# A hybrid recurrent layer with sixteen experts: the second expert's token gather placed ahead of the overflow branch

## The chip, the cores and the metric

The kernel runs on one core of a Trainium2 chip. The metric is the device time of one execution, in microseconds. Engines are named as in the profile: PE (TensorE, its weight loads PEld apart), DVE (VectorE), ACT (ScalarE), POOL (GpSimd) and SP (SyncE, which here issues most DMAs).

## The reference

One layer over 512 latent tokens of 1024 channels (and 256 context tokens that only feed the recurrences): a modulated norm, an input projection, two groups of four recurrent heads, an output projection with a gated residual, and then a mixture of sixteen experts, of which each token takes the two best of its best group of four. A final norm follows. The part around the change is this:

```python
xs = xs + g1x * (ox @ w_out[l])
xs = xs + g2x * hierarchical_moe(modulate(rms_norm(xs, norm2_w[l]), sh2x, sc2x), *moe_args)
...
g_idx = jnp.argmax(g_logits, axis=-1)
top_v, top_i = lax.top_k(e_in_group, TOP_K_IN_GROUP)
expert_id = g_idx[:, None] * EXPERTS_PER_GROUP + top_i
...
for e in range(N_EXPERTS):
    a = jax.nn.silu(t @ w_gate[e]) * (t @ w_up[e])
    y = y + gates[:, e:e + 1] * (a @ w_down[e])
...
return rms_norm(xs, final_norm_w)
```

Everything is float32. The expert weights are 16 x 3 matrices of 2 MB.

## The kernel before

**Stages.** Up to about 545 us the kernel makes the modulation, the input projection and the two recurrences. The output projection runs in two halves of 512 channels: the first (L1278) for all four token tiles of 128, the second (L1336) tile by tile. Behind each tile of the second half DVE adds the residual (`residual`, L1219 to L1236; the add is L1224), PE turns the tile channel-major and makes the 20 router logits (L1250), and DVE adds and scales them (L1254, L1255). `Routing.route` (L99) picks the two experts of each token and their positions in the experts' lists, for tiles 0 and 1 first and then for tiles 2 and 3.

**Token rows.** `token_rows(t)` (L1260 to L1269) makes the normed and modulated rows of tile t in two DVE instructions (a multiply L1266 by the broadcast `a2`, a multiply-add L1267 with `sh2`) and writes them to `t_d`, a buffer in device memory, in one DMA of 512 KB (L1268). Tiles 0 and 1 are made during the output projection and written from SP's queue; tiles 2 and 3 are made later and written from POOL's queue (`t >= RA`, RA is 2).

**Slot tables.** `Routing.finish` (L198) builds the table that says which token sits in which of 128 slots of each expert: eight one-hot tiles on DVE (`collect`, L176), eight small matmuls into `s0ps` (L177), and five short DVE instructions (`table`, L182 to L186) that end in the row numbers.

**Expert 0** takes its tokens by matmuls with one-hots (L1290, L1296), then gets its scale and shift in `x0` (L1408 on DVE, L1410 on ACT), and runs the gate and up products in float32 (L1424). All other experts take their tokens by an indirect DMA (`gather`, L1370 to L1373) from `t_d`: it needs all four tiles of rows and the table. The gather of expert 1 is L1371 on POOL.

**The overflow branch.** The largest count of tokens of an expert is loaded into a register (L1431), and `tc.If(over > P)` (L1432) branches over a loop for experts with more than 128 tokens. Every engine takes part in the branch, and where it is skipped each engine's queue still raises the semaphores that the skipped code would have raised. `branch` (L1477) is the branch's place in the program; weight loads written after it are held behind it.

**Experts 1 to 15.** `up(e)` transposes the gathered rows on PE (L1501), splits them into a high and a low part (`xh` on ACT, `xl` on DVE), and makes gate (`pg`) and up (`pu`) products of 24 reduced-precision matmuls each (L1513). `down(e)` does the same for the down projection (`at` L1531, `ah` on ACT L1535, `al` on DVE L1536, `py` L1544). The weights are split the same way, high on ACT (L1393) and low on DVE (L1398), into four buffers each. `gated` (L1524) is the activation between them; the first one after the branch needs a table load on ACT. `down` of expert e-1 stands between the two products of expert e.

**Weight loads.** `load_weights` (L1198 to L1207) issues 96 loads of 1 MB from SP's queue in the order of a list, `(expert, piece)` with pieces 0 and 1 gate, 2 and 3 up, 4 and 5 down. The raw tiles rotate through 12 buffers of three pools (a string, `turns`, says which). Ten loads are issued ahead of the branch, five in the output projection and five after the mixer's buffers are free; three more stand right behind the branch in the program, and the rest as buffers come free.

**What sets the order.** A scheduler places instructions on the engines by priority and dependencies. `tc.issue_after(i)` and `tc.add_manual_dep(..., behind, ...)` keep an instruction behind another in the order, and `hi(1000)` raises priority. The two late broadcast loads, `g2b` (the gate of the second residual, L1488) and `fw` (the final norm's weight, L1490), 512 KB each, reuse the buffers of `a2` and `sh2`, and so wait until the last token rows are made.

## Time and profile before

| | |
|---|---|
| median of 3 runs | 979.87 us (977.32 to 984.05) |
| the profiled execution | 978.06 us |
| its span, first to last instruction | 976.3 us |
| mean granted TensorE clock | 0.958 of full speed |
| PE busy | 875.8 us (90%) |
| PEld busy | 717.4 us (73%) |
| DVE busy | 732.7 us (75%) |
| ACT busy | 499.6 us (51%) |
| POOL busy | 216.4 us (22%) |
| DMA moved | 180.03 MB, mean 184 GB/s |

Times in the trace are counted from the start of the span. The profiled execution is 1.8 us longer than its span, and 1.8 us below the median. In rows of the timeline a bracket gives the idle time of the engine in front of the instruction and what ended it; in rows of windows the numbers are the window, its length, the busy time and instruction count of PE, PEld, DVE, ACT and POOL, the granted clock, the busy share of the DMA engines and GB/s. A clock of 1.00 is 2.4 GHz, 0.50 is 1.2 GHz.

### The profile page before, as it was taken

The page shows a single profiled execution, that of the slowest core. Times are in us where ns is not written, and L with a number is a line of the kernel's source. Part 1 is how long each engine was busy: PE and PEld are TensorE (multiplying, and loading weights), DVE is VectorE, ACT ScalarE, POOL GpSimd, SP SyncE. Part 2 cuts the span into 40 slices and gives each one's busy share as a digit, 9 for nine tenths or more (in the row PEclk, how much of TensorE's full clock was granted, in tenths as well). Part 3 has the DMA queues.
Part 4 walks back from the last instruction along what each step waited for, and adds up shares of the span by engine and source line. Part 5 has one row for each costly group of instructions (what it writes and reads, how often), then busy time and mean ns, then how long its engine had stood idle before and what let it go on. Part 6 is the DMA issues. An engine that isn't in the chain of part 4 may idle for free.

```text
span 976.3 us, 20470 instructions
## 1 busy us (share of the span) xinstructions
PE 875.8 (90%) x8205; PEld 717.4 (73%) x8205; DVE 732.7 (75%) x1378; ACT 499.6 (51%) x958; POOL 216.4 (22%) x226
## 2 busy tenths in 40 slices
PE   3999998989789998799999979859999999999971
PEld 1688887878678887777877768638888877777750
DVE  2698499747899589945475656748899888888877
ACT  4435542554345344433523423317888887887841
POOL 2232621252145204311112100011111111010041
PEclk9899997999899999999999999979999999999985
DMA  9921350201002111057136393579999999999342
GB/s 309 307 65 31 124 171 25 78 11 46 24 22 66 33 37 34 11 185 219 55 132 195 112 357 140 216 255 387 368 361 367 370 368 370 369 377 372 136 185 86
DMA packets 115436, 180.03 MB, mean 184 GB/s; under 512 B 9863, under 2 KB 49347, under 8 KB 114824
## 3 DMA queue, kind: packets, MB, share of 16 engines
q1 hardware_dynamic: 108392, 163.76, 49.0%
q0 software_dynamic: 6192, 13.66, 3.8%
q8 instruction: 66, 1.08, 0.4%
q10 hardware_dynamic: 752, 1.25, 0.3%
q14 instruction: 34, 0.28, 0.1%
HBM read 170.31 MB, written 16.27 MB: 191 GB/s over the span
## 4 chain that ended last, share of the span: by engine, by line
PE 65%; DVE 17%; DMA 8%; issue 5%; ACT 4%; SPq 1%; POOL 1%; POOLq 0%; ACTq 0%; DVEq 0%
PE pu L1513 8%; PE py L1544 8%; PE pg L1513 8%; PE hf_1pl L457 2%; PE hf_0pl L457 2%; PE wo L1336 2%; DMA wm<-in_w_mod_dram 2%; DVE vc L562 2%; PE psm L1003 1%; DVE KS L938 1%; PE hi1p L856 1%; PE z11p L856 1%; PE hf_1pc L463 1%; DVE lo L1398 1%; PE z01p L856 1%
## 5 line engine op out<-in xcount | busy, mean ns | idle before, releaser
L1398 DVE TENSOR_TENSOR lo<-w,hi 128x1024 fp32r<-128x1024 f32 x184 | 216.3, 1221 | 27.1 <-ACT hi L1393 25.4
L1393 ACT CAST hi<-w 128x1024 fp32r<-128x1024 f32 x184 | 185.1, 1050 | 20.3 <-PE pu L1513 8.8
L1544 PE MATMUL py<-lo,ah 128*128 128x512 f32 x128 | 52.5, 410 | 1.0 <-DVE lo L1398 0.6
L1544 PE MATMUL py<-hi,ah 128*128 128x512 f32 x128 | 51.3, 402 | 0.7 <-ACT ah L1535 0.7
L1544 PE MATMUL py<-hi,al 128*128 128x512 f32 x128 | 49.9, 399 | 0.0
L1513 PE MATMUL pg<-lo,xh 128*128 128x512 f32 x120 | 49.1, 409 | 0.0
L1513 PE MATMUL pu<-lo,xh 128*128 128x512 f32 x120 | 48.4, 403 | 0.0
L1513 PE MATMUL pg<-hi,xh 128*128 128x512 f32 x120 | 48.2, 402 | 0.0
L1513 PE MATMUL pg<-hi,xl 128*128 128x512 f32 x120 | 47.7, 398 | 0.0
L1378 POOL DMA_INDIRECT y_d<-y,cl x15 | 17.2, 1148 | 136.9 <-ACT y L1546 123.4
L1513 PE MATMUL pu<-hi,xh 128*128 128x512 f32 x120 | 47.6, 396 | 0.0
L1513 PE MATMUL pu<-hi,xl 128*128 128x512 f32 x120 | 47.3, 394 | 0.0
L815 POOL TENSOR_TENSOR am<-atr,cst 128x128 f32<-128x128 f32 x32 | 17.7, 557 | 122.2 <-PE po L818 107.3
L1371 POOL DMA_INDIRECT xg<-t_d,cl x15 | 17.7, 1181 | 120.5 <-PE xt L1501 110.6
L938 DVE TENSOR_TENSOR KS<-KS,F 128x384 f32<-128x384 f32 x56 | 32.2, 613 | 3.3 <-ACT km L901 2.8
L1544 PEld LDWEIGHTS py<-lo,ah 128*128 128x128 f32 x128 | 24.5, 191 | 9.8 <-DVE lo L1398 4.5
L811 DVE TENSOR_SCALAR vs<-px,bs 128x128 f32<-128x128 f32 x48 | 16.5, 344 | 18.9 <-PE px L809 18.7
L562 DVE SCALAR_TENSOR_TENSOR qc<-lpad,cw,qc 128x512 f32<-128x512 f32 x32 | 29.3, 917 | 0.4
L1544 PEld LDWEIGHTS py<-hi,ah 128*128 128x128 f32 x128 | 24.5, 191 | 6.8 <-ACT ah L1535 0.9
L1544 PEld LDWEIGHTS py<-hi,al 128*128 128x128 f32 x128 | 24.3, 190 | 5.7 <-DVE al L1536 0.3
L1513 PEld LDWEIGHTS pu<-lo,xh 128*128 128x128 f32 x120 | 22.5, 188 | 7.9 <-DVE lo L1398 3.0
L1003 PE MATMUL psm<-wm,cl 128*32 128x128 f32 x512 | 25.2, 284 | 3.2 <-DMA wm<-in_w_mod_dram 3.0
(1058 smaller groups left out, 2717.4 us busy)
## 6 DMA issues: line engine op xcount, KB each, us to landing
w<-in_w_gate_dram SPq DMA_DIRECT2D x32, 1024.0 KB, 15.0
w<-in_w_up_dram SPq DMA_DIRECT2D x32, 1024.0 KB, 15.0
w<-in_w_down_dram SPq DMA_DIRECT2D x32, 1024.0 KB, 14.9
wm<-in_w_mod_dram SPq DMA_DIRECT2D x64, 256.0 KB, 4.0
wm<-in_w_mod_dram SPq DMA_DIRECT2D x16, 512.0 KB, 8.1
y_d<-zt POOLq DMA_DIRECT2D x8, 512.0 KB, 8.1
wor<-in_w_out_dram SPq DMA_DIRECT2D x8, 512.0 KB, 4.6
yv<-y_d SPq DMA_DIRECT2D x4, 1024.0 KB, 10.9
```

The lines of the kernel that those rows point to most:

```text
L457: nc.tensor.matmul(pl, w[:, kb % 4, :], hh[:, kb, CTX:], start=st, stop=sp)
L562: nc.vector.scalar_tensor_tensor(al, s, w, al, op0=ALU.mult, op1=ALU.add)
L815: nc.gpsimd.tensor_mul(am, atr[:, t, :], K(("le", "ge")[d]))
L856: nc.tensor.matmul(ps[:, 0:256], hh[:, kb, i * P:(i + 1) * P], w[:, kb % 2, :], start=(kb == 0 and n == 0), stop=(kb == KB - 1 and n == 2))
L938: nc.vector.tensor_mul(kh, kh, tt(d, 1 - d))
L1003: nc.tensor.matmul(ps[32 * c_:32 * c_ + 32, P * j:P * j + P], cl[:, kb, :], raw[:, P * c_:P * c_ + P], start=(kb == 0), stop=(kb == KB - 1))
L1336: put(nc.tensor.matmul(acc1, m[:, kb, ts_], w[:, kb % 2, :], start=(i == 0 and n == 0), stop=(i == KB - 1 and n == 2)))
L1371: return nc.gpsimd.indirect_dma_start(out=dst, out_offset=None, in_=t_d[:, :], in_offset=bass.IndirectOffsetOnAxis(ap=idx, axis=0), bounds ...
L1393: nc.scalar.copy(hi, raw)
L1398: s.append(lo_on.tensor_sub(s[1], raw, s[0].bitcast(F32)))
L1513: nc.tensor.matmul(ps, m[:, kb, :], ww[:, k, :], start=(kb == 0 and n == 0), stop=(kb == KB - 1 and n == 2))
L1544: nc.tensor.matmul(ps, m[:, k, :], ww[:, k % 2, :], start=(k == 0 and n == 0), stop=(k == 3 and n == 2))
```

## The change

Four things are moved; no arithmetic changes.

1. The rows of tile 2 are made inside the output projection, behind the position sums of tiles 0 and 1 (`summed`), and written from SP's queue; the residual add of tile 3 is kept behind them. Only tile 3's rows are left for later, on POOL's queue.
2. `finish` (the eight slot one-hots and the table) is written ahead of `x0`, and DVE's part of `x0` is kept behind the last one-hot (`hot`).
3. The gather of expert 1 (`picked`) is kept ahead of the branch, which is ordered behind it. Four weight loads, (2,0), (2,1), (1,4) and (1,5), are written ahead of the branch, and the three behind it are gone.
4. `a2` and `sh2` get tiles of their own, and `g2b` and `fw` are loaded right behind the first five weight loads, during the output projection.

```diff
@@ Routing
-            nc.vector.tensor_add(self.pre[:, t + 1, :], self.pre[:, t, :], self.sel[:, t, :])
+            self.summed = nc.vector.tensor_add(self.pre[:, t + 1, :], self.pre[:, t, :], self.sel[:, t, :])
...
-            nc.vector.tensor_scalar(O, self.K("iota"), self.pos[:, k, t:t + 1], None, op0=ALU.is_equal)
+            self.hot = nc.vector.tensor_scalar(O, self.K("iota"), self.pos[:, k, t:t + 1], None, op0=ALU.is_equal)
@@ tile_kernel
-    sh2 = late.tile([P, D], F32, tag="fw", name="sh2")
-    a2 = late.tile([P, D], F32, tag="g2b", name="a2")
+    sh2 = rt.tile([P, D], F32, name="sh2")
+    a2 = rt.tile([P, D], F32, name="a2")
...
     with tc.issue_after(last_wo.ins):
         for i in range(NR1):
-            load_weights()
+            ld = load_weights()
+    g2b = late.tile([P, D], F32, name="g2b")
+    fw = late.tile([P, D], F32, name="fw")
+    with tc.issue_after(ld.ins):
+        nc.sync.dma_start(g2b, mod_d[3].partition_broadcast(P))
+        nc.sync.dma_start(fw, final_norm_w.partition_broadcast(P))
...
-    def residual(nh, t, acc):
+    def residual(nh, t, acc, made=None):
...
-            nc.vector.tensor_add(xv, xv, acc)
+            added = nc.vector.tensor_add(xv, xv, acc)
+            if t == NLT - 1:
+                tc.add_manual_dep(added.ins, made.ins.name, behind, reason="behind the rows")
...
-        (nc.gpsimd if t >= RA else nc.sync).dma_start(t_d[t * P:(t + 1) * P, :], tt_)
+        (nc.gpsimd if t > RA else nc.sync).dma_start(t_d[t * P:(t + 1) * P, :], tt_)
...
         if t == RA:
             tables.route(lg, 0, RA)
+            with tc.issue_after(tables.summed.ins):
+                made = token_rows(t)
             tables.first_slots(Oe, 0, RA, 0, ssx[:, 3, :])
...
+    with hi(1000), tc.issue_after(weighed.ins):
+        ix0, ws0 = tables.finish(xg[1].rearrange("p (n s) -> p n s", n=2 * NLT), cl)
+    slots = tables.put
...
+        if kb % 2:
+            tc.add_manual_dep(x0v.ins, tables.hot.ins.name, behind, reason="behind the slots")
     with hi(1000), tc.issue_after(x0v.ins):
-        ix0, ws0 = tables.finish(xg[1].rearrange("p (n s) -> p n s", n=2 * NLT), cl)
-        for t in range(RA, NLT):
-            made = token_rows(t)
-    gather(xg[1], ix0[:, 1, 1:2])
-    slots = tables.put
+        made = token_rows(NLT - 1)
+    picked = gather(xg[1], ix0[:, 1, 1:2])
...
+    for i in range(4):
+        load_weights()
...
     branch = nc.cur_bb.bb.instructions[-1]
+    tc.add_manual_dep(branch, picked.ins.name, behind, reason="behind the second expert's tokens")
     mw2 = moe.enter_context(tc.tile_pool(name="mw2", bufs=1, side="right"))
-    for i in range(3):
-        load_weights()
...
-    g2b = late.tile([P, D], F32, tag="g2b", name="g2b")
-    nc.sync.dma_start(g2b, mod_d[3].partition_broadcast(P))
-    fw = late.tile([P, D], F32, tag="fw", name="fw")
-    nc.sync.dma_start(fw, final_norm_w.partition_broadcast(P))
```

The orders below show three places. In the changed kernel line numbers are some ten higher: the token rows' DMA L1268 is L1276, the gather L1371 is L1382, `x0` L1408 is L1422, the low splits L1398 are L1409, the branch L1432 is L1448.

POOL's queue around the branch, in the kernel before (`t_d` the token rows' buffer, `tt` the rows, `cnti` the largest count, `xeo` the gather inside the skipped loop):

```order
L1164 COPY shb<-col_7428 128x1024
L1236 TENSOR_TENSOR B_163<-B_163,half 128x1 x4
L1268 DMA t_d<-tt_8104 128x1024 x2
L1431 TENSOR_LOAD cnti
L1432 COMPARE_AND_BRANCH
L1435 COMPARE_AND_BRANCH
```

and in the changed kernel:

```order
L1164 COPY shb<-col_7428 128x1024
L1244 TENSOR_TENSOR B_163<-B_163,half 128x1 x4
L1276 DMA t_d<-tt_7878 128x1024
L1382 DMA xg_8071<-t_d,cl 128x1024
L1447 TENSOR_LOAD cnti
L1448 COMPARE_AND_BRANCH
```

One of the two writes of rows has left the queue, and the gather into `xg_8071` now stands ahead of the register load and the branch; before, it came after the branch's end.

DVE's queue from the end of the routing weights to the low splits of expert 1's first weights (`xg_8062` holds `x0`, `xg_8063` the one-hots, `cl` the slot table), in the kernel before:

```order
L1408 TENSOR_SCALAR xg_8062<-xT_0_7938,A_162 128x128
L1408 TENSOR_SCALAR xg_8062<-xT_1_7939,A_162 128x128
L1408 TENSOR_SCALAR xg_8062<-xT_0_7938,A_162 128x128
L1408 TENSOR_SCALAR xg_8062<-xT_1_7939,A_162 128x128
L176 TENSOR_SCALAR xg_8063<-cst,pos 128x128 x8
L1266 TENSOR_TENSOR tt_8104<-xs_7386,a_7476 128x1024 x2
L1267 SCALAR_TENSOR_TENSOR tt_8104<-tt_8104,B_163,sh_7475 128x1024 x2
L182 TENSOR_SCALAR cl<-s0ps,cst 128x16
L183 SCALAR_TENSOR_TENSOR cl<-s0ps,cl 128x16
L186 COPY cl<-s0ps 128x16
L184 CAST cl<-cl 128x16
L185 TENSOR_SCALAR cl<-cl 128x16
```

and in the changed kernel (`xg_8070` holds `x0`, `xg_8071` the one-hots):

```order
L176 TENSOR_SCALAR xg_8071<-cst,pos 128x128 x8
L1422 TENSOR_SCALAR xg_8070<-xT_0_7946,A_162 128x128
L1422 TENSOR_SCALAR xg_8070<-xT_1_7947,A_162 128x128
L1422 TENSOR_SCALAR xg_8070<-xT_0_7946,A_162 128x128
L1422 TENSOR_SCALAR xg_8070<-xT_1_7947,A_162 128x128
L1274 TENSOR_TENSOR tt_7878<-xs_7386,a_7476 128x1024
L182 TENSOR_SCALAR cl<-s0ps,cst 128x16
L1275 SCALAR_TENSOR_TENSOR tt_7878<-tt_7878,B_163,sh_7475 128x1024
L183 SCALAR_TENSOR_TENSOR cl<-s0ps,cl 128x16
L186 COPY cl<-s0ps 128x16
L184 CAST cl<-cl 128x16
L185 TENSOR_SCALAR cl<-cl 128x16
```

The eight one-hots stand ahead of `x0` in place of behind it, one pair of row instructions is gone from here, and the first instruction of the table stands between the two that are left.

SP's queue from the fifth weight load to the branch, in the kernel before (`w_0` to `w_5` are pieces of an expert's weights, the number behind them tells the tile):

```order
L1204 DMA w_0_7490<-in_w_gate_dram 128x4x512
L1268 DMA t_d<-tt_7717 128x1024 x2
L1204 DMA w_1_8064<-in_w_gate_dram 128x4x512
L1204 DMA w_4_8066<-in_w_down_dram 128x4x512
L1204 DMA w_5_8068<-in_w_down_dram 128x4x512
L1204 DMA w_2_8070<-in_w_up_dram 128x4x512
L1204 DMA w_3_8072<-in_w_up_dram 128x4x512
L1431 TENSOR_LOAD cnti
L1431 ISA x2
L1488 DMA g2b<-mod_d 128x1024
L1490 DMA fw<-in_final_norm_w_dram 128x1024
L1432 COMPARE_AND_BRANCH
```

and in the changed kernel from the first row writes on (`g2b` and `fw` stand directly in front of them):

```order
L1276 DMA t_d<-tt_7721 128x1024 x2
L1204 DMA w_4_8156<-in_w_down_dram 128x4x512
L1276 DMA t_d<-tt_7878 128x1024
L1204 DMA w_1_8072<-in_w_gate_dram 128x4x512
L1204 DMA w_4_8074<-in_w_down_dram 128x4x512
L1204 DMA w_5_8076<-in_w_down_dram 128x4x512
L1204 DMA w_2_8078<-in_w_up_dram 128x4x512
L1204 DMA w_3_8080<-in_w_up_dram 128x4x512
L1447 TENSOR_LOAD cnti
L1447 ISA x2
L1204 DMA w_0_8152<-in_w_gate_dram 128x4x512
L1448 COMPARE_AND_BRANCH
```

The broadcast loads `g2b` and `fw` stand ahead of the token rows, the rows of tile 2 and the load (1,4) (`w_4_8156`) ahead of the five loads of the second batch, and the load (2,0) (`w_0_8152`) ahead of the branch in place of `g2b` and `fw`.

## Rows read from the trace of the kernel before

**Rows 1.** Windows: one row per stretch of the program.

```profile
583.00:617.00 34.00, 32.40 (x187) 27.53 (x185) 21.23 (x60) 10.06 (x22) 1.64 (x3) 1.00 0.35 133
...
630.00:646.00 16.00, 16.00 (x53) 8.05 (x52) 13.98 (x30) 5.17 (x8) 1.20 (x2) 1.00 0.53 182
646.00:656.50 10.50, 0.05 (x1) 0.00 (x0) 0.69 (x1) 1.88 (x2) 2.11 (x2) 0.61 0.82 299
...
675.00:900.00 225.00, 224.23 (x1027) 179.59 (x1027) 200.72 (x197) 186.09 (x220) 28.50 (x24) 1.00 1.03 369
```

**Rows 2.** Timeline of PE: the start of expert 1.

```profile
656.51 1.97 PE L1501 MATMUL xt<-cst,xg 128*128 128x128 f32 x8 [10.45 <-DMA xg<-t_d,cl]
658.98 0.78 PE L1513 MATMUL pg<-hi,xh 128*128 128x512 f32 x1
```

**Rows 3.** Chain of waits from 600 to 670 us: start, length, step.

```profile
638.94 8.53 DMA t_d<-tt
...
649.12 7.34 DMA xg<-t_d,cl
...
659.33 6.84 PE pg L1513 x24
```

**Rows 4.** Timeline of ACT behind the branch.

```profile
646.82 1.28 ACT L1524 ACT_TABLE_LOAD   x1 [11.09 <-PEq L1432]
648.12 0.60 ACT L1524 ACTIVATE a<-pg 128x512 f32<-128x512 f32 x1
```

**Rows 5.** Timeline of DVE from the last tile's residual to the first low splits.

```profile
614.60 0.18 DVE L1254 TENSOR_TENSOR lg<-plg,lgp 128x20 f32<-128x20 f32 x1 [1.14 <-PE plg L1250]
...
616.53 0.69 DVE L1224 TENSOR_TENSOR xs<-xs,wo 128x512 f32<-128x512 f32 x1 [1.40 <-PE wo L1336]
...
630.17 0.41 DVE L1408 TENSOR_SCALAR xg<-xT,A 128x128 f32<-128x128 f32 x1 [1.52 <-ACT xg L1410]
632.33 1.65 DVE L176 TENSOR_SCALAR xg<-cst,pos 128x128 f32<-128x128 f32 x8
633.89 2.35 DVE L1266 TENSOR_TENSOR tt<-xs,a 128x1024 f32<-128x1024 f32 x2
636.16 2.48 DVE L1267 SCALAR_TENSOR_TENSOR tt<-tt,B,sh 128x1024 f32<-128x1024 f32 x2
...
639.32 4.62 DVE L1398 TENSOR_TENSOR lo<-w,hi 128x1024 fp32r<-128x1024 f32 x4
```

**Rows 6.** Issue to landing by source line: rows L1268, gathers L1371, loads L1204 of 610 to 625 us.

```profile
DMA to landing us min/median/max: 4.0/6.2/8.5
...
DMA to landing us min/median/max: 7.0/7.4/8.2
...
DMA to landing us min/median/max: 5.4/13.3/14.8
```

**Rows 7.** Timeline of SP around the branch.

```profile
636.27 0.35 SPq L1488 DMA_DIRECT2D g2b<-mod_d  x1
...
646.55 0.94 SPq L1204 DMA_DIRECT2D w<-in_w_gate_dram  x2
```

**Rows 8.** Windows in which PE stood idle, and one between the loads.

```profile
622.50:624.60 2.10, 0.05 (x1) 0.02 (x1) 1.86 (x14) 0.00 (x0) 0.00 (x0) 1.00 1.05 407
...
634.00:636.00 2.00, 2.00 (x15) 1.53 (x13) 2.00 (x2) 1.74 (x2) 0.00 (x0) 1.00 0.00 0
646.00:648.00 2.00, 0.05 (x1) 0.00 (x0) 0.00 (x0) 1.18 (x1) 0.00 (x0) 1.00 0.15 44
```

**Rows 9.** Chain that ended last: up products of experts 2, 8 and 14.

```profile
691.00 4.20 PE pu L1513 x18
...
799.61 5.81 PE pu L1513 x24
...
912.09 5.81 PE pu L1513 x24
```

**Rows 10.** Waits from 781 to 976 us: total, times, longest.

```profile
ACT ah L1535 <- PE at L1531: 20.1, 9, 2.4
```

More of the change, by code (lines that the diff above doesn't have):

```diff
@@ L1207, in load_weights @@
         raws[e, n] = t
+        return ld
     with tc.issue_after(last_wo.ins):
         for i in range(NR1):
-            load_weights()
+            ld = load_weights()
[4 more added lines that the diff above has]
+        nc.sync.dma_start(fw, final_norm_w.partition_broadcast(P))
     t_d = dr.tile([SEQ, D], F32, name="t_d")
@@ L1325, in part @@
             logits(nh, t, tTs[nh, t], put)
+    made = None
     for t in range(NLT):
@@ L1338, in tile_kernel @@
         with hi(1000):
-            residual(1, t, acc1)
+            residual(1, t, acc1, made)
         if t < RA:
```

## Prediction

> **What bounds the kernel now.** I read the windows by stage first: they tell where an engine that otherwise works all the time stands still. PE is busy for all of the 16.00 us from 630 to 646, for 0.05 of the next 10.50 us, and for 224.23 of 225.00 us in the loop over the experts [rows 1]. The reader is to see one hole, from 646.05 (end of expert 0's up product) to 656.51, and behind it a loop in which time can be saved only by a better order on PE or by other durations. In the same hole the clock falls: its mean is 0.61, while it is 1.00 before.
>
> PE's timeline names what ends the hole: the transposes of expert 1 waited 10.45 us for the gather, and its first gate matmul starts at 658.98, 2.47 us after them [rows 2]. The chain of waits gives what is behind the gather. The row write of tile 3 was issued at 638.94 and took 8.53 us, so it landed at 647.47; the gather was issued 1.65 us later, at 649.12, and took 7.34 us [rows 3]. ACT's timeline is the second thing that can end last there: after the branch it loads a table (646.82, 1.28 us) and runs expert 0's activation (0.60 us, to 648.72) [rows 4], and only then the split of expert 1's tokens. So ACT leaves room for about 8 us of an earlier gather, and no more. DVE's timeline shows why the row write is so late: one-hots, two multiplies and two multiply-adds of rows stand in a line from 632.33 to 638.64, right behind `x0` [rows 5].
>
> **The change part by part.** All times are of the profiled execution.
>
> *The gather's start.* DVE stands idle for 1.52 us in front of the second `x0` instruction, which waits for PE and ACT [rows 5]. The eight one-hots need 1.65 us and now stand ahead of `x0`; they fill that gap, so `x0` ends as before, at 632.4. Behind it stand one multiply (half of 2.35, 1.2 us), a short table instruction (0.2) and one multiply-add (half of 2.48, 1.25): the rows of tile 3 are ready at about 635.0 in place of 638.6. The write is issued 0.3 us later, as before (638.64 to 638.94), at 635.3, which is 3.6 us earlier.
>
> *Its landing.* The two writes from POOL took 4.0 and 8.5 us [rows 6]: the first when the DMA engines had little else, the second with the first, `g2b` (issued 636.27, [rows 7]) and `fw` behind `g2b` beside it. These three are gone from its side, and the DMA engines moved nothing from 634 to 636 [rows 8], though the weight loads now end about 1 to 2 us later, as the rows of tile 2 (0.5 MB) stand ahead of them on SP. I take 4.0, nearest to a lone write, and keep 8.5 for the range: landed at 639.3. The gather follows 1.65 us later as before, at 641.0; the fifteen gathers take from 7.0 to 8.2 [rows 6] and I keep 7.34. The tokens arrive at 648.3, while ACT is at 648.7. The 2.47 us from the transposes to the first gate matmul stay: 650.8 in place of 658.98. That is 8.2 us less.
>
> The Trainium skill's page "DMA: Bandwidth & Descriptors" (section "Anatomy of one DMA — SWDGE (gpsimd) path") fits a transfer from that queue as 2.0 us plus its bytes over 436e3 per us; for 512 KB an estimate of 3.2 us. The gathers' rows say 7.0 at the least [rows 6], so I don't use it. By it the tokens would come 4 us before ACT is ready and the gain would be about 1 us more.
>
> *The clock behind the hole.* The 24 gate matmuls at 659.33 took 6.84 us; the up products of the loop take 5.81 [rows 3, 9]. PE now stands idle from 646.05 to 648.3, 2.25 us. In two idle stretches of 2.10 and 2.00 us the granted clock was 1.00 [rows 8], so I count the slow start as gone: 1.0 us for those matmuls and an estimated 0.2 for the transposes, 1.2 us. The bounds are 0 and 1.2.
>
> *The loop's order.* Adding loads and the gather ahead of the branch shifts what the scheduler does in the loop. It runs experts in two patterns. From expert 2's up product (691.00) to expert 8's (799.61) an expert takes 18.10 us, from there to expert 14's (912.09) 18.75 [rows 9]; in the second one `ah` stands ahead of two weight splits on ACT. In the new order the first pattern lasts one expert longer and one expert is mixed, so 1 to 2 of the 6 slow intervals go: 0.65 to 1.3 us, and I take 1.0.
>
> *The rows of tile 2.* The multiply and multiply-add (2.4 us) now stand on DVE ahead of and between the logits' instructions at 614.60, which waited 1.14 us, and the residual add at 616.53, which waited 1.40 us [rows 5]. Both gaps make 2.54 us, so nearly all is hidden; I charge 0.3 us for the last tile's residual, and 1.2 at the most (one of the two instructions not covered).
>
> *The loads.* `g2b`, `fw` and load (1,4) go from behind the branch to stretches in which the DMA engines are busy for 0.35 of the time [rows 1]; they delay nothing that is waited for. Of the other three early loads (2,0) is issued at about 638 in place of 646.55 and (2,1) and (1,5) stay behind the branch on SP; nothing waits for these weights, since PE waits for nothing in the loop [rows 1]. If that cover were gone, 2 MB at the loop's 369 GB/s [rows 1] would be 5.7 us, but of load time alone. The freed buffers for `a2` and `sh2`, and the DMA writes' change of queue for tile 2, cost nothing: SP has only loads behind that write, of which the first was issued at 616.5 and waits about 1 us more. The branch now waits for the gather's issue on POOL alone (641.0), before PE reaches it. Nothing of the change touches the time after the last expert.
>
> Sum: 8.2 + 1.2 + 1.0 - 0.3 = 10.1 us, 968.0 of 978.06 in the profiled execution's time. The median is 1.8 us above that execution; by ratio (0.9897) the median comes to 969.8.
>
> **The rivals.**
>
> *The row write straggles again.* It is still on POOL's queue. If it takes 8.5 us beside the last weight loads, it lands at 643.8, the gather at 652.8, the first gate matmul is at 655.3: 3.7 us less, with a hole of 6.8 us and a slow clock behind it. 3.7 + 1.0 - 0.3 = 4.4, 973.7, or 975.5 on the median. For it speaks that one of the two writes took that long; against it, that the other took 4.0 and the DMA engines are idle when the write starts. The same page of the Trainium skill ("Latency and other measured facts") says that DMA engines 7 and 15 are usually slower and guesses at the descriptor rings of the software queue as the cause; no row here separates the engines. By it this rival would hold on idle engines too.
>
> *The branch waits for the load (2,0).* SP passed the branch only when its loads had landed (its next load is at 646.55, 10.3 us after `g2b` was issued, [rows 7]). Now a 1 MB load stands there, issued once the first two low splits are done, about 638.2. Such a load took 5.4 us when first in line and 13.3 at the median [rows 6]. At 5.4 it has landed at 643.6 and costs nothing. At 13.3 it lands at 651.5; ACT's table load is then at 651.9, and the first gate matmul at about 655.1, with a slow clock: 3.9 + 1.0 - 0.3 = 4.6, or 975.3 on the median. Against it: few loads are ahead of it.
>
> *The loads set the pace of the loop.* DMA is busy all through it (share 1.03, 369 GB/s, [rows 1]). If the loop ends with the loads, the gain is that of the two loads taken out of it, 5.7 us: 974.2. Against it: PE waits for nothing in 224 of 225 us there.
>
> *Slower: the new order stalls each expert.* On ACT `ah` waited for PE's transposes 20.1 us in nine waits, the longest 2.4 [rows 10], with weight splits queued behind it. If the new order put two of them in the way in all 13 intervals, at twice the loss of the slow pattern, 1.3 us each, that is 16.9 us, of which 3.9 are there today: +13.0 against 8.2 + 1.2 - 0.3 = 9.1, so 982.0, or 983.8. It decides from 1.0 us per interval. Against it: the new order shows the two known patterns.
>
> **How the numbers follow.** Forecast 0.64; straggling write 0.15; load at the branch 0.09; loads set the pace 0.06; slower 0.06. A difference of 1% (9.8 us) is about what a measurement of this kernel can tell from no change. My forecast lies just beyond it; as a larger share of short idle or a kinder order in the loop also counts there, I give it 0.42 of faster and 0.22 of same. The rivals between 974 and 976 add 0.30 to same: 0.52; slower by over 1% is 0.06. The range: below, an earlier gather (ACT has room for 0.8 us more), all six slow intervals gone (3.9 in place of 1.0) and no loss at the rows (0.3) make 4.0 us more, 965.8, and the runs before lie up to 2.5 us under their median, which I add for the measurement's part: 963.3. Above, the straggling write at 975.5 without the loop's 1.0 us and with 0.9 us more for tile 2's rows makes 977.4, and 0.6 us for a gather of 8.2 us beside it in part: 978.0.
>
> **What would show it.** Right: the profile afterwards has the row write at 635 with 4 to 5 us to landing, the gather issued at 640 to 641, the transposes at about 648, and a granted clock near 1.00 through 646 to 660; up products of experts 2 to 9 18.1 us apart. The gather at 644 or later means the straggle; SP's first load behind the branch, and ACT's table load, at 650 or later mean the load; an end of the hole 8 us earlier with a total only 5 us shorter means the loads; intervals above 19 us mean the slower case. Wrong would be the whole account if the gather came by 648 and PE still waited for something else until 655.

## The result, and the profile after

| | before | after |
|---|---|---|
| median | 980.73 us (4 runs, 977.32 to 984.05) | 970.26 us (4 runs, 967.03 to 971.5) |
| ratio of the runs | | 0.9888, 95% interval 0.9846 to 0.9931 |
| the profiled execution, span | 976.3 us | 969.7 us |
| mean granted TensorE clock | 0.958 | 0.964 |

The kernel is 1.1% faster (0.7 to 1.5%); forecast were 969.8 us and a ratio of 0.9897. The two spans differ by 6.6 us only, and that has to be explained before anything is read from them. DVE's timeline has one instruction early in the output projection, before all that the change moves, that serves as a mark. In the kernel before and in the changed one it stands at

```profile
576.64 0.18 DVE L1169 TENSOR_TENSOR cb<-pcb,rb 128x20 f32<-128x20 f32 x1 [3.04 <-PE pcb L1167]
```

```profile
581.92 0.18 DVE L1169 TENSOR_TENSOR cb<-pcb,rb 128x20 f32<-128x20 f32 x1 [3.10 <-PE pcb L1167]
```

So the profiled execution of the changed kernel came 5.28 us late to a place that it reaches by the same work. In the profiles of the experiments below this mark lies anywhere from 574.20 to 579.12; three of these kernels differ from the changed one only in places far behind it and reach it at 574.20, 575.74 and 577.08. A scatter of several us so comes from ahead of all that the change moves. All traces are therefore compared from a second mark, the end of expert 0's up product: 646.05 before, 651.33 after (also 5.28 apart, so nothing was won or lost between the marks). From there to the end of the span it is 330.25 us before and 318.37 after: 11.9 us less. Two experiments have a disturbed profiled execution (2840 and 1664 us); of these only the times of the other runs are used.

PE's timeline of the changed kernel behind that mark (start, length, instruction, and in brackets the idle time before it; it answers to [rows 2]):

```profile
646.87 4.46 PE L1437 MATMUL pu<-w,xg 128*128 128x512 f32 x10
651.47 1.07 PE L1512 MATMUL xt<-cst,xg 128*128 128x128 f32 x8
654.23 0.65 PE L1542 MATMUL at<-cst,a 128*128 128x128 f32 x4 [1.69 <-DVE a L1536]
654.64 0.48 PE L1524 MATMUL pg<-hi,xh 128*128 128x512 f32 x1
```

The transposes `xt` no longer wait for the gather: they run 0.14 us after the up product. The hole from there to the first gate matmul is 3.31 us, where it was 12.93, and what ends it is another engine's work. The chain that ended last says whose:

```profile
651.56 1.28 ACT L1535
...
652.86 0.61 ACT a L1535
...
653.49 0.70 DVE a L1536
...
654.23 0.65 PE at L1542 x4
654.88 5.60 PE pg L1524 x24
```

It is ACT's table load behind the branch, the activation of expert 0, DVE's product, PE's transposes of it, and then the gate product, whose 24 matmuls take 5.60 us where they took 6.84 [rows 3]. The windows (columns as in [rows 1]) show why: PE's idle time is short and the clock stays at 1.00, where it was 0.61 on the mean.

```profile
646.00:656.50 10.50, 8.66 (x33) 4.91 (x32) 2.92 (x6) 3.61 (x6) 2.24 (x3) 1.00 0.80 276
...
675.00:900.00 225.00, 224.27 (x1037) 180.54 (x1036) 200.58 (x196) 186.32 (x222) 28.59 (x23) 1.00 1.03 370
```

POOL's timeline, and the landings of the row writes and of the gathers (they answer to [rows 3, 6]):

```profile
640.45 0.64 POOL L1276 DMA_DIRECT2D t_d<-tt  x1 [15.84 <-DVE cl L184]
644.73 1.51 POOL L1382 DMA_INDIRECT xg<-t_d,cl  x1 [3.64 <-DVE tl L1498]
```

```profile
DMA to landing us min/median/max: 2.6/3.0/3.2
...
DMA to landing us min/median/max: 5.3/7.5/8.3
```

The write of tile 3 was issued 10.88 us ahead of the mark (7.11 before), landed within 3.2 us (8.53 before), and the gather was issued 6.60 us ahead of the mark, where it had come 3.07 us behind it. The view of this gather alone has

```profile
DMA to landing us min/median/max: 5.3/5.3/5.3
```

so the tokens were there at 650.0, 1.3 us ahead of the mark. DVE's timeline shows the one-hots in front of `x0` and the rows of tile 2 in their gap (answering to [rows 5]):

```profile
618.65 1.22 DVE L1274 TENSOR_TENSOR tt<-xs,a 128x1024 f32<-128x1024 f32 x1
619.87 0.18 DVE L1262 TENSOR_TENSOR lg<-plg,lgp 128x20 f32<-128x20 f32 x1
619.98 1.28 DVE L1275 SCALAR_TENSOR_TENSOR tt<-tt,B,sh 128x1024 f32<-128x1024 f32 x1
621.18 0.23 DVE L1263 SCALAR_TENSOR_TENSOR lg<-lg,B,cb 128x20 f32<-128x20 f32 x1
621.79 0.69 DVE L1230 TENSOR_TENSOR xs<-xs,wo 128x512 f32<-128x512 f32 x1 [0.38 <-PE wo L1345]
...
633.83 1.65 DVE L176 TENSOR_SCALAR xg<-cst,pos 128x128 f32<-128x128 f32 x8
635.44 0.41 DVE L1422 TENSOR_SCALAR xg<-xT,A 128x128 f32<-128x128 f32 x1
```

DVE's residual add at 621.79 still waited 0.38 us for PE, so the rows of tile 2 cost nothing at all. Last, the loop: up products of experts 2, 8, 10 and 14 in the chain (answering to [rows 9]):

```profile
685.30 4.20 PE pu L1524 x18
...
793.94 4.20 PE pu L1524 x18
...
830.76 5.81 PE pu L1524 x24
...
905.66 5.81 PE pu L1524 x24
```

An expert takes 18.11 us from 2 to 8 and 18.73 from 10 to 14. The two intervals between can't be read from these rows, as one piece of the chain has the last 18 of the 24 matmuls and the other all of them; from end to end of the up products they are 18.3 and 18.7. Five slow intervals and a mixed one are left, where there were six and a mixed one. From the first gate matmul of expert 1 to the end it is 317.32 us before and 315.06 after, 2.26 less. The gate matmuls' clock makes 1.24 of it. The loop makes 0.8: from the end of expert 1's up product to that of expert 15's, PE's timeline has 257.45 us before (678.25 to 935.70) and 256.70 after (672.56 to 929.26).

### The profile page after: what moved, and what is told of

Its sections match the earlier page's. It is cut to its first block, busy times and chain, and to the rows that moved or that the text cites. A ratio compares the mean times of both kernels' runs of the same rounds, so it can differ in the third digit from the quotient of the medians.

```text
span 969.7 us, 20466 instructions
## 1 busy us (share of the span) xinstructions
PE 879.4 (91%) x8205; PEld 720.3 (74%) x8205; DVE 732.4 (76%) x1378; ACT 500.8 (52%) x958; POOL 217.8 (22%) x225
## 5 line engine op out<-in xcount | busy, mean ns | idle before, releaser
L1409 DVE TENSOR_TENSOR lo<-w,hi 128x1024 fp32r<-128x1024 f32 x184 | 216.7, 1221 | 26.6 <-ACT hi L1404 24.9
L1382 POOL DMA_INDIRECT xg<-t_d,cl x15 | 19.5, 1303 | 114.3 <-PE xt L1512 104.5
L938 DVE TENSOR_TENSOR KS<-KS,F 128x384 f32<-128x384 f32 x56 | 29.7, 569 | 3.3 <-ACT km L901 2.8
L562 DVE SCALAR_TENSOR_TENSOR vc<-lpad,cw,vc 128x512 f32<-128x512 f32 x32 | 29.8, 931 | 0.3
```

Source lines behind the costliest of these rows:

```text
L562: nc.vector.scalar_tensor_tensor(al, s, w, al, op0=ALU.mult, op1=ALU.add)
L938: nc.vector.tensor_mul(kh, kh, tt(d, 1 - d))
L1382: return nc.gpsimd.indirect_dma_start(out=dst, out_offset=None, in_=t_d[:, :], in_offset=bass.IndirectOffsetOnAxis(ap=idx, axis=0), bounds ...
L1409: s.append(lo_on.tensor_sub(s[1], raw, s[0].bitcast(F32)))
```

## The experiments

All measure two stretches of the profiled execution: the hole (end of expert 0's up product to the first gate matmul of expert 1), and the rest from that matmul to the span's end. "Cold" says that the first gate matmul took 0.78 us in place of 0.48. The rest also holds the stretch behind expert 15's up product, at which no edit aims; it takes from 39.0 to 41.4 us in these traces, so differences of about 1 us in the rest mean little by themselves.

| kernel | hole | rest | ratio to before (95%) |
|---|---|---|---|
| before | 12.93 cold | 317.3 | |
| the changed kernel | 3.31 | 315.1 | 0.9888 (0.9846 to 0.9931) |
| gather behind the branch | 3.32 | 315.3 | 0.9873 (0.9836 to 0.9911) |
| gather ahead, alone | not read | not read | 0.9990 (0.9969 to 1.0012) |
| early broadcast loads, alone | 9.56 cold | 316.7 | 0.9970 (0.9936 to 1.0004) |
| without tile 2's early rows and early weight loads | 6.59 cold | 317.7 | 0.9949 (0.9924 to 0.9975) |
| without early weight loads | 3.32 | 318.2 | 0.9920 (0.9894 to 0.9947) |
| without tile 2's early rows | 9.37 cold | 316.1 | 0.9953 (0.9926 to 0.9979) |
| broadcast and weight loads late | 6.77 cold | 317.8 | 0.9942 (0.9910 to 0.9974) |
| broadcast loads late | not read | not read | 0.9992 (0.9969 to 1.0014) |
| all weight loads ahead of SP's branch | 8.32 cold | 317.8 | 0.9945 (0.9925 to 0.9965) |
| table loaded early | 2.05 | 315.0 | 0.9884 (0.9851 to 0.9916) |
| table early, one order in the loop | 2.05 | 310.7 | 0.9822 (0.9776 to 0.9867) |

**Is it the gather's place?**

```diff
-    picked = gather(xg[1], ix0[:, 1, 1:2])
...
-    tc.add_manual_dep(branch, picked.ins.name, behind, reason="behind the second expert's tokens")
+    picked = gather(xg[1], ix0[:, 1, 1:2])
+    tc.add_manual_dep(picked.ins, branch.name, behind, reason="behind the branch")
```

> The changed kernel, with the gather of expert 1 alone put back behind the branch. Theory (the hole between expert 0's up product and expert 1's first gate product is what was saved, and the early gather is what saves it): POOL comes past the branch about 0.7 us after expert 0's up product ends, the gather then takes 5.3 to 7.5 us, the first gate product starts 9 to 10.5 us after that product's end in place of 3.3, and its 24 matmuls take 6.8 us in place of 5.6. Slower than the changed kernel by 7 to 9 us, so 0.996 to 0.998 of the kernel before. Rival (the gain comes from the loads that were taken from behind the branch): the gather's place matters little and the ratio stays at 0.988 to 0.990.

The theory failed here: the kernel is as fast as the changed one, as the rival had it. (The rival's reason, the loads, is tested below and turns out to be a part of the gain.) POOL's rows at the branch and its timeline:

```profile
L1447 POOLq COMPARE_BRANCH  x1: 53/53/53, 634.5 to 634.5; - x1
```

```profile
633.82 0.64 POOL L1276 DMA_DIRECT2D t_d<-tt  x1 [15.83 <-DVE cl L184]
638.10 1.51 POOL L1382 DMA_INDIRECT xg<-t_d,cl  x1 [3.64 <-DVE tl L1498]
```

POOL took its branch at 634.5, 10.2 us ahead of the end of the up product (644.69), and the gather went out at 638.10, 6.59 us ahead of it as in the changed kernel. Each engine goes through the branch in its own time, and POOL is through at once, with the row write of 633.82 (3.0 us to landing) still in flight. What held the gather in the kernel before was the row write alone, as [rows 3] had it. The trace of the kernel before shows the same:

```profile
L1432 POOLq COMPARE_BRANCH  x1: 53/53/53, 640.2 to 640.2; - x1
```

POOL took its branch there 7.3 us before the row write was down (647.47), so its own queue did not hold the gather there either.

The opposite, the kernel before with the gather alone put ahead:

```diff
-    gather(xg[1], ix0[:, 1, 1:2])
+    picked = gather(xg[1], ix0[:, 1, 1:2])
...
     branch = nc.cur_bb.bb.instructions[-1]
+    tc.add_manual_dep(branch, picked.ins.name, behind, reason="behind the second expert's tokens")
```

> The kernel before, with the gather of expert 1 alone put ahead of the branch. Theory: the gather still waits for the row write of tile 3, which lands 8.5 us after its issue, 1.4 us behind the end of expert 0's up product; the hole stays 9.5 to 10.5 us and the ratio is 0.998 to 1.003. Rival (the place of the gather in POOL's queue is the whole of it): the hole shrinks to about 3.3 us as in the changed kernel, and the ratio is 0.990.

0.9990 (0.9969 to 1.0012): no difference that the times can tell, as the theory had it, and not the rival's 0.990. The hole itself is on no trace that could be read. In neither kernel is the place of the gather in POOL's queue worth anything measurable.

**What made the row write late: the staircase.** From the kernel before, the parts were added one at a time. First the broadcast loads:

```diff
-    sh2 = late.tile([P, D], F32, tag="fw", name="sh2")
-    a2 = late.tile([P, D], F32, tag="g2b", name="a2")
+    sh2 = rt.tile([P, D], F32, name="sh2")
+    a2 = rt.tile([P, D], F32, name="a2")
...
+    with tc.issue_after(ld.ins):
+        nc.sync.dma_start(g2b, mod_d[3].partition_broadcast(P))
+        nc.sync.dma_start(fw, final_norm_w.partition_broadcast(P))
```

> The kernel before, with one part of the change alone: g2b and fw get buffers of their own and are loaded during the output projection. Theory (these loads ran beside the row write of tile 3 and made it slow): its landing 3.5 to 5 us in place of 8.5, the first gate product of expert 1 8 to 9.5 us behind the end of expert 0's up product in place of 12.9, with a slow clock behind it as before; ratio to before 0.995 to 0.997. Rival (the second of two row writes on POOL's queue is slow in any company): landing 7 to 8.5 us, hole 11.5 to 12.9 us, ratio 0.998 to 1.001.

Row writes' landing, and PE's wait:

```profile
DMA to landing us min/median/max: 2.6/3.3/5.5
```

```profile
655.63 1.97 PE L1503 MATMUL xt<-cst,xg 128*128 128x128 f32 x8 [7.08 <-DMA xg<-t_d,cl]
```

The longest landing falls from 8.5 to 5.5 us and the hole from 12.93 to 9.56, 3.4 us for this part. The theory holds in kind, with landing and hole just above what it allowed (5 and 9.5); the time alone (0.9936 to 1.0004) would not show it. What is left of the straggle has two companions that this run does not part: the other row write, and a weight load that SP now issued in the place of `g2b`.

Then the one-hots ahead of `x0` (and the gather ahead, for which nothing was found), which is the changed kernel less two parts:

```diff
-            with tc.issue_after(tables.summed.ins):
-                made = token_rows(t)
...
-        made = token_rows(NLT - 1)
+        for t in range(RA, NLT):
+            made = token_rows(t)
...
-    for i in range(4):
-        load_weights()
...
+    for i in range(3):
+        load_weights()
```

> The changed kernel, without the early rows of tile 2 and without the early weight loads: the early broadcast loads, the slots ahead of x0 and the early gather stay. Theory: the one-hots ahead of x0 bring the row write 1.5 us forward against the broadcast loads alone; hole 6.5 to 8 us, slow clock behind it, ratio to before 0.993 to 0.996. With ACT held by nothing but PE (table load 0.3 us behind the up product's end). Rival (the row write of tile 2 in front of it in POOL's queue costs nothing, as only its issue counts): hole 5 to 6 us.

The hole is 6.59 us, 3.0 less than with the broadcast loads alone; 1.5 were expected of the earlier issue, which came 1.42 us earlier against the mark; the landing gave nearly as much again (4.2 in place of 5.5). Then tile 2's rows, by leaving out the early weight loads alone:

```diff
-    for i in range(4):
-        load_weights()
...
+    for i in range(3):
+        load_weights()
```

> The changed kernel, with the four early weight loads taken back and three written behind the branch, as before. Theory (they only change the order in the loop): the hole stays 3.3 us; from expert 2's first product on six slow experts in place of five, 0.6 to 1.3 us slower; ratio to before 0.989 to 0.991. Rival (the loads set the pace of the loop): two loads more behind the branch, up to 5.7 us slower, ratio 0.993 to 0.995.

The hole is 3.32, that of the changed kernel, so tile 2's rows, put last, are worth another 3.3 us and a clock of 1.00 behind the hole. The weight loads do nothing in the hole, as both sides had it, but the rest is 3.1 us longer, more than the 0.6 to 1.3 expected and less than the rival's 5.7. It splits so: 1.4 us from the first gate matmul to the end of expert 2's up product, 0.8 from there to the end of expert 15's (six slow intervals in place of five, as expected), and 1.0 behind that, where the traces scatter that much. For the first part PE's timeline has

```profile
668.41 1.03 PE L1511 MATMUL xt<-cst,xg 128*128 128x128 f32 x8
...
671.13 0.60 PE L1511 MATMUL xt<-cst,xg 128*128 128x128 f32 x4
674.81 0.60 PE L1511 MATMUL xt<-cst,xg 128*128 128x128 f32 x4
```

Expert 3's transposes are torn in two and stand within expert 2's gate product, and PE waits for DVE there. From 655 to 697 us PE, ACT and DVE wait for each other only, and for no load, so this is an order that the scheduler chose. The theory holds in kind (order, not pace: the last experiment below wins time on the same loads as the changed kernel), but one place of the order cost 1.4 us, about as much as two slow experts.

Taking away tile 2's rows alone from the changed kernel gives another picture:

```diff
-            with tc.issue_after(tables.summed.ins):
-                made = token_rows(t)
...
-        made = token_rows(NLT - 1)
+        for t in range(RA, NLT):
+            made = token_rows(t)
```

> The changed kernel, with the rows of tile 2 back behind x0 and on POOL's queue, as before. Theory (the row write of tile 3 is late by the 2.4 us of tile 2's rows on DVE and a little slower behind another write): its issue is 2.2 to 2.6 us later against the picks, its landing 3 to 5 us, the first gate product 0 to 4 us later than in the changed kernel, as 2 us of the gather's lead are not needed; ratio to before 0.989 to 0.993. Rival (a second write in POOL's queue is what makes the straggle): landing 6 to 8.5 us, first gate product 5 to 7 us later, ratio 0.994 to 0.997.

The ratio came out above the expected one and the hole is 9.37 us, 2.8 longer than in the step of the staircase that has the same rows. The rival's numbers fit (6.1 us later, 0.9953), but not its cause, as the write landed in 4.2 us and not in 6 to 8.5. ACT's timeline and SP's semaphores behind its branch (first and last start) say why:

```profile
651.12 1.28 ACT L1532 ACT_TABLE_LOAD   x1 [16.26 <-DMA xg<-t_d,cl]
```

```profile
L1445 SPq EVENT_SEMAPHORE  x8: 17/17/17, 646.5 to 651.0; - x8
```

In this order the scheduler puts three weight loads ahead of SP's branch, and ACT starts when SP's last semaphore is raised at 651.0, though PE had ended at 645.18. Neither theory nor rival of this run had named this; it is the rival of the prediction that has the branch wait for a load, and was tested by itself.

**Does the branch wait for loads?**

```diff
-    for i in range(4):
-        load_weights()
+    ahead = [load_weights() for i in range(4)]
...
+    for ld in ahead:
+        tc.add_manual_dep(branch, ld.ins.name, behind, reason="behind the loads")
```

> The changed kernel, with all four early weight loads ahead of SP's branch, in place of two. Theory A (ACT goes past the branch only when SP's loads have landed): ACT's table load starts 2 to 6 us later than the end of expert 0's up product, the first gate product 5 to 9 us behind it in place of 3.3; ratio to before 0.991 to 0.996. Theory B (what slows the start of expert 1 is the row write's landing alone): table load 0.2 us behind the up product, hole 3.3 us, ratio 0.988 to 0.990.

SP's timeline and semaphores, and ACT:

```profile
637.03 1.06 SPq L1204 DMA_DIRECT2D w<-in_w_gate_dram  x2
638.19 0.45 SPq L1204 DMA_DIRECT2D w<-in_w_down_dram  x1
650.32 0.38 SPq L1204 DMA_DIRECT2D w<-in_w_gate_dram  x1
```

```profile
L1447 SPq EVENT_SEMAPHORE  x8: 17/17/17, 645.3 to 650.2; - x8
```

```profile
650.30 1.28 ACT L1536 ACT_TABLE_LOAD   x1 [15.20 <-DMA xg<-t_d,cl]
```

Theory A holds: three loads were issued by 638.64, the last of them landed at 649.9, SP's last semaphore came at 650.2, and ACT's table load follows 0.1 us later, 4.9 us behind the up product (645.41). The row write and the gather are issued as early as in the changed kernel, so theory B falls. In the changed kernel only the load (2,0) stands there, and its row has room to spare:

```profile
L1448 SPq EVENT_SEMAPHORE  x8: 17/17/17, 648.4 to 649.0; - x8
```

SP was through at 649.0, 2.3 us ahead of PE.

**The broadcast loads put back.** Two kernels; the first leaves the early weight loads in, the second takes both back:

```diff
-    sh2 = rt.tile([P, D], F32, name="sh2")
-    a2 = rt.tile([P, D], F32, name="a2")
+    sh2 = late.tile([P, D], F32, tag="fw", name="sh2")
+    a2 = late.tile([P, D], F32, tag="g2b", name="a2")
...
-    with tc.issue_after(ld.ins):
-        nc.sync.dma_start(g2b, mod_d[3].partition_broadcast(P))
-        nc.sync.dma_start(fw, final_norm_w.partition_broadcast(P))
```

> The changed kernel, with g2b and fw back in the buffers of a2 and sh2 and loaded behind the last rows; SP then issues them and three weight loads ahead of its branch. Theory: the row write of tile 3 was slow before because these loads ran beside it (then its landing goes from 3 us back to 6 to 8.5 us), and ACT goes past the branch only once SP's loads have landed, 4 to 10 us later than in the changed kernel. First gate product 3 to 10 us later; ratio to the kernel before 0.993 to 0.999. Rival (the row write is slow only beside a second row write in the same queue, and a landing at the branch costs nothing): landing stays 3 to 4 us, the hole stays 3.3 us, ratio 0.988 to 0.990.

All of the gain is gone (0.9992), as the theory had it. This run mixes two causes, the company of the row write and three weight loads at the branch, and without a trace that can be read it can't say how they share. Its sister separates them:

> The changed kernel, with g2b and fw late in the old buffers, and the early weight loads back behind the branch, so that SP has only g2b and fw ahead of its branch. Theory (the loads beside it slow the row write of tile 3): landing 6 to 8.5 us in place of 3, the gather issued 4 to 6 us later, the first gate product 7 to 9 us behind the end of expert 0's up product in place of 3.3, a slow clock behind it; ratio to the kernel before 0.994 to 0.998. Rival (the run with broadcast loads late lost its gain only because three weight loads had to land before ACT came past the branch): landing 3 to 4 us, hole 3.3 us, ratio 0.989 to 0.991.

The row writes' landing, and PE's wait:

```profile
DMA to landing us min/median/max: 2.7/3.1/6.5
```

```profile
651.04 1.97 PE L1510 MATMUL xt<-cst,xg 128*128 128x128 f32 x8 [4.29 <-DMA xg<-t_d,cl]
```

6.5 us in place of 3, a hole of 6.77 (7 to 9 were expected), the gather 3.6 us later against the mark (4 to 6 expected) and a cold product. The theory holds, a little smaller than expected: the kernel without the early weight loads differs from this one by the broadcast loads alone and has a longest landing of 3.0 us and a hole of 3.32, so it is the two loads beside it that make the write of the last rows slow.

**What ends the hole now.**

```diff
-            nc.scalar.copy(hi, raw)
+            hcopy.append(nc.scalar.copy(hi, raw))
...
+    warm = late.tile([P, 1], F32, name="warm")
+    with tc.issue_after(hcopy[-1].ins):
+        nc.scalar.activation(warm, half[:, 0:1], AF.Silu)
```

> The changed kernel, with one activation of a single column put on ACT ahead of the branch, so that the table is loaded there and not behind it. Theory (ACT's chain behind the branch sets the end of the hole that is left): ACT's activation of expert 0 starts 1.28 us earlier, and so does the first gate product, 2.0 us behind the up product's end in place of 3.3; about 0.13% faster than the changed kernel, ratio to before 0.987. Rival (the gathered rows or PE's own transposes set it): the first gate product starts at most 0.3 us earlier.

ACT and PE in the trace of this kernel:

```profile
645.42 0.60 ACT L1539 ACTIVATE a<-pg 128x512 f32<-128x512 f32 x1 [9.06 <-PEq L1452]
```

```profile
647.21 0.48 PE L1528 MATMUL pg<-hi,xh 128*128 128x512 f32 x1
```

No table load stands behind the branch any more, and the hole is 2.05 us, 1.26 less: the theory. In the ratio (0.9884) so little can't be told from nothing.

**The loop's order.** To this the order of the fast pattern was added for the later experts (rows of the down product's split, and the activation, kept behind the weight splits):

```diff
+        if 8 <= e < NE - 1:
+            for n, h in ((4, 0), (4, 1), (5, 0)):
+                w5 = weights(e, n, h)
+            h50 = hcopy[-1]
-        nc.scalar.copy(ah, pv)
-        nc.vector.tensor_sub(al, pv, ah.bitcast(F32))
+        ah_ = nc.scalar.copy(ah, pv)
+        al_ = nc.vector.tensor_sub(al, pv, ah.bitcast(F32))
+            tc.add_manual_dep(ah_.ins, h50.ins.name, behind, reason="behind the split")
+            tc.add_manual_dep(al_.ins, w5[2].ins.name, behind, reason="behind the split")
...
+                tc.add_manual_dep(xh_.ins, ahs[e - 2].ins.name, behind, reason="behind the rows")
...
+                tc.add_manual_dep(acts[e - 1].ins, xh_.ins.name, behind, reason="behind the next rows")
+                tc.add_manual_dep(h51[e - 2].ins, xh_.ins.name, behind, reason="behind the next rows")
```

> The changed kernel with the activation table loaded ahead of the branch and, from expert 8 on, the order of ACT and DVE kept to that of experts 2 to 7 (the split of the down product's rows behind three of the four weight splits). Theory (the slow pattern costs 0.65 us per expert by its order alone): all intervals 18.1 us, 3 to 3.9 us less than with the table alone, 1.3 us less for the table; ratio to before 0.983 to 0.985. Rival (the later experts are slow because buffers or loads come late there): intervals of experts 9 to 14 stay 18.7 us or more, ratio 0.987 to 0.988.

Up products of experts 8 and 14 in its chain, and the window of the later experts:

```profile
787.78 4.20 PE pu L1534 x18
...
896.30 4.41 PE pu L1534 x19
```

```profile
800.00:900.00 100.00, 100.00 (x462) 81.16 (x461) 90.55 (x89) 85.45 (x100) 12.46 (x10) 1.00 1.03 374
```

The second piece begins one matmul (0.21 us) earlier in its product than the first, so six intervals make 108.73 us, 18.12 each. The rest is 4.3 us shorter than with the table alone: 3.4 from the end of expert 1's up product to that of expert 15's, within the 3 to 3.9 expected, and 0.9 behind it, where the traces scatter that much. The slow pattern is a matter of order, and the weight loads had at least 3.4 us in hand. At 0.9822 (962.08 us median) this is the fastest of the kernels, ahead of both.

## Why the prediction was right

*The hole.* The row write was forecast 3.6 us earlier and came 3.77 us earlier against the mark. Its landing was taken at 4.0 and took 3.0; the gather followed 1.3 us later and not 1.65, and landed after 5.3 us and not 7.34. So the tokens came 1.3 us ahead of the mark, where they were forecast 2.25 us behind it, and the hole ends with ACT, which the prediction named as second in line. What the change saved in the hole was 9.6 us where 8.2 were forecast. The 1.4 us between are not the transfers', which are off the path now. About 0.5 is ACT's own start, for which 0.77 us behind the up product was kept from before and 0.23 came. PE's semaphore behind the branch shows it, before and after:

```profile
L1432 PEldq EVENT_SEMAPHORE  x1: 51/51/51, 646.6 to 646.6; - x1
```

```profile
L1448 PEldq EVENT_SEMAPHORE  x1: 51/51/51, 651.4 to 651.4; - x1
```

It came 0.5 us behind the up product before and 0.1 after, and ACT 0.2 us behind it both times; why PE was late before, no run shows. The other 0.9 is the wrong path: the prediction kept 2.47 us from the transposes `xt` to the first gate matmul and hung them on the tokens' arrival, but they ran under ACT's table load, and from the end of ACT's activation (653.46) it is 1.2 us to the first gate matmul.

*The clock.* Forecast 1.2 us, found 1.24 (6.84 to 5.60), with a granted clock of 1.00 through the shorter hole. The equal sums are in part luck: 1.0 was taken for the matmuls, from a product of the slow pattern (5.81), and 0.2 for the transposes, which are off the path now. The reason given, that two idle stretches of about 2 us left the clock at 1.00 [rows 8], is weaker than it looked. The first of them lies between the matmuls of the routing, and in three of the experiments' traces the granted clock fell to 0.50 (1.2 GHz) around that place. Those are the kernels with the gather behind the branch, without early weight loads, and without these and tile 2's early rows; the stretch between the two marks took 70.4 to 70.6 us there in place of 69.4. One window of the kernel without early weight loads, behind an idle stretch of 2.06 us:

```profile
628.00:632.00 4.00, 4.00 (x28) 4.00 (x28) 3.14 (x25) 0.65 (x5) 0.00 (x0) 0.73 1.05 383
```

All five holes of 2.05 to 3.32 us in the table kept 1.00, and all of 6.59 us and more did not.

*The loop.* Forecast 1.0, found 0.8, by the way that was forecast: one slow interval less. That it is order and not pace is shown from both sides: with the early weight loads taken back the loop takes 2.2 us more, though PE, ACT and DVE wait 0.3 us in all for loads there, and with another order on the same loads 3.4 us are won.

*Tile 2's rows.* 0.3 us were charged, nothing was found between the marks. Their gain stands in the prediction without a price of its own, as a shorter line on DVE and a write less beside tile 3's. Taken in this order, the staircase gives 3.4 us to the broadcast loads, 3.0 to the one-hots and 3.3 to these rows; in another order the shares could differ. The ratios, which rest on all runs, fall from step to step too (0.9970, 0.9949, 0.9920, and 0.9888 with the early weight loads), but their intervals overlap: the shares are read from one trace each.

The sum of 10.1 us stands against 11.9 in the trace from the mark on and 11.0 by the ratio (1 less 0.9888, of 980.73). The mechanism is the one forecast; the hole was sized 1.4 us too small, tile 2's rows 0.3 too dear and the loop 0.2 too large, and 0.3 of the trace's gain belongs to none of the terms.

*The rivals.* The straggling write did not come; the trace has 3.0 us. The cause that the prediction gave for it, the company of `g2b` and `fw`, is shown from both sides (8.5 to 5.5 by moving them alone, 3.0 to 6.5 by moving them back). The load at the branch is a true mechanism that missed its condition: with (2,0) alone SP was through 2.3 us ahead of PE; with three loads the hole is 8.32, close to the 9.0 that the rival had priced (655.1 against 646.05). That the loads set the pace is refuted by the last experiment, and of stalls in each interval the chain shows none.

What the prediction left unsaid is that the part which the title names is empty. Its sum was built on the row write, rightly, and gave no price to the gather's place; but a reader could take it that the early place was needed. It is not.

## What to carry to other kernels

Before a transfer is moved ahead of a branch, look at what it waits for: here its own queue was never the wait, and the data that it reads was. A chain through several transfers is shortened by taking away what runs beside its slowest link, and loads without a deadline are the first to go. Once such a hole is closed, the next engine in line ends it, here a table load that one dummy instruction moves out of the way; and the order that a scheduler finds differs by 2 to 3 us from one edit to the next, as much as a part of the change.

## What was not expected of the hardware

Each engine goes through a skipped branch at its own time: POOL 10.2 us ahead of PE's end (634.5), with its own row write still in flight and its next transfer out 6.6 us ahead of that end. But ACT started only behind the later of PE and SP: the table load began 0.1 us after SP's last semaphore where SP was late (650.2 to 650.30) and 0.23 us after PE's end where SP was early (651.33 to 651.56). And SP's last semaphore came 0.3 to 0.5 us behind the landing of the last load that it had issued ahead of the branch (649.9 and 650.2 with three loads, 648.5 and 649.0 with one).

Row writes of 512 KB landed in 2.6 to 3.2 us in the changed kernel, where no other write and no broadcast load is beside them, in 4.2 to 5.5 right behind another one, in 6.5 beside two broadcast loads and in 8.5 with both. The Trainium skill's page "DMA: Bandwidth & Descriptors" (section "Anatomy of one DMA — SWDGE (gpsimd) path") gives an estimate of 3.2 us for this size by its fit, which the lone write from POOL's queue, at 3.0 us, bears out; the gathers of the same size, at 5.3 to 8.3 us with weight loads beside them, do not follow it.
